# Row sums of a 32x512x1024 tensor: one or two loads issued ahead of the opening barriers

## Chip, cores and metric

The kernel runs on one core of a Trainium2 chip. The metric is the device time of one execution in microseconds (us). Before the change it is 160.77 us, the median of 3 runs (160.69 to 160.84).

## What is computed

```python
def reference(x: np.ndarray) -> np.ndarray:      # x: float32 (32, 512, 1024)
    return np.sum(x, axis=-1).astype(np.float32)
```

64 MB are read, 64 KB are written: 16,384 rows of 1024 numbers are summed, each to one number.

## The kernel before

The 16,384 rows are spread over 128 partitions, 128 rows for each, cut into three blocks of 32, 48 and 48 rows for a partition (`BLOCKS`). Within a block each partition's rows are contiguous in memory. A block is worked off in groups of 16 rows (`G`), eight groups in all, so a full group is a tile of 128 partitions x 16,384 numbers, 64 KB for a partition and 8 MB in all. Three such buffers (`xt`) are used in turn, so the load of group b+3 must wait until the sums of group b are done.

All loads are issued by SyncE (SP), from a list `loads` (L90 to L103) that is worked off in one loop (L146 to L149). The list begins with two loads for group 0: the first row alone (`LEAD`, 4 KB for a partition, 512 KB in all, semaphore `first`) and the other fifteen rows (60 KB for a partition, 7,680 KB, semaphore `slot0`). Groups 1 to 6 follow, one load each, and then the last group in smaller pieces: 9, 4 and 2 rows into its `xt` buffer, and its last row in two parts into `tail`. Group b's load, from b = 3 on, waits for VectorE's counter `vec` (L148). All these loads go through one DMA queue, and 16 DMA engines share each of them, 8 partitions to an engine.

VectorE sums the rows of a group with one `tensor_reduce` (L63): one row first (L110, after `first`), then the other fifteen of group 0 (L115, after `slot0`), then 16 at a time; ScalarE (L74) takes 7 rows of the seventh group and half of each of the last pieces. The last row is summed by two instructions at L81. The results leave by three stores (L155) and a last one (L159), issued by SP.

The program that is built has an entry part and a body. In the entry part GpSimd (POOL) sets four constants, and all engines meet in barriers (the profile gives the first of them L208, and two more L169): each engine drains, adds to a semaphore that Pool waits for, and then waits for Pool's release. The body, with everything above, comes behind them, after a branch. The end of the kernel (L175 to L194) edits this order by hand: it takes the first `EARLY` DMA instructions of SP out of the body and puts them in the entry part, ahead of SP's first drain:

```python
    loads = [i for i in code if i.engine == sp and i.opcode == "DMACopy"][:EARLY]
    for load in loads:
        assert not load.sync_info.on_wait
        code.remove(load)
    body.instructions = code
    code = list(entry.instructions)
    at = next(k for k, i in enumerate(code) if i.engine == sp and i.opcode == "Drain")
    code[at:at] = loads
```

With `EARLY = 2` these are the two loads of group 0.

Of the kernel before, what the change touches and what calls it, by code (L numbers as in the profile page):

```python
# [13 lines left out]
ACT_ROWS = 7  # L14
CUT = 544
CUTS = (0, 9, 13, 15)
EARLY = 2


def row_sums(nc, x: bass.AP, out: bass.AP):  # L20
# [146 lines left out]
def kernel(tc: tile.TileContext, x: bass.AP, out: bass.AP):  # L167
# [17 lines left out]
    code = list(body.instructions)  # L185
    loads = [i for i in code if i.engine == sp and i.opcode == "DMACopy"][:EARLY]
    for load in loads:
# [36 lines left out]
```

## Time and profile before

| what | value |
|---|---|
| median of 3 runs | 160.77 us |
| the profiled execution's own time | 160.73 us |
| its span in the trace | 159.4 us |
| read from memory | 67.11 MB, 421 GB/s over the span |
| one-row load, issue to landing | 3.5 us |
| 15-row load, issue to landing | 21.2 us |
| VectorE, sum of 16 rows (128x16,384) | 17.22 us |
| VectorE, sum of 15 rows | 16.15 us |
| VectorE's longest wait, for the 15-row load | 16.9 us |

The span runs from the first instruction in the trace, SP's first DMA issue, to the last one. SP's own column in the profile (SPq) shows how long it takes to issue a DMA; the transfer itself follows on the DMA engines, and "landing" is when its semaphore has its full count. An engine name with a q is that engine's sequencer, where waits and barriers are handled.

### The profile page before, as it was taken

How to read it: one execution, taken by the hardware profiler on the slowest of the kernel's cores; microseconds unless marked ns; L12 is line 12 of the kernel's file. 1: busy time of each engine (PE TensorE's matmuls, PEld its weight loads, DVE VectorE, ACT ScalarE, POOL GpSimd, SP SyncE). 2: the span in 40 equal slices, each digit the busy share in tenths (PEclk: the TensorE clock that was granted, in tenths of full speed). 3: DMA queues.
4: the chain of work that ended last, by engine and by line, in shares of the span. 5: the costliest groups of instructions: out<-in, count | busy, mean ns of one | idle time of the engine just before them, and what ended most of it. 6: DMA issues, size and time to landing. Idle time of an engine off the chain costs nothing.

```text
span 159.4 us, 110 instructions
## 1 busy us (share of the span) xinstructions
DVE 121.5 (76%) x17; ACT 17.2 (11%) x31; POOL 0.2 (0%) x4
## 2 busy tenths in 40 slices
DVE  1100059994799968999499994999949999499685
ACT  3000000000000000000000000000000000494694
POOL 0000000000000000000000000000000000000000
DMA  9988996996997989969969969969979799699994
GB/s 378 493 370 370 493 526 263 526 526 263 526 477 312 526 378 411 526 263 526 526 263 526 526 263 526 526 263 526 460 329 526 312 477 526 296 444 444 387 400 151
DMA packets 2448, 67.18 MB, mean 421 GB/s; under 512 B 784, under 2 KB 912, under 8 KB 1168
## 3 DMA queue, kind: packets, MB, share of 16 engines
q1 hardware_dynamic: 2448, 67.18, 98.2%
HBM read 67.11 MB, written 0.07 MB: 421 GB/s over the span
## 4 chain that ended last, share of the span: by engine, by line
DMA 75%; DVE 22%; SPq 1%; issue 0%
DMA xt<-in_x_dram 50%; DMA tail<-in_x_dram 25%; DVE res L63 22%; SPq L149 1%; DVE pairs L81 0%; DVE res L81 0%
## 5 line engine op out<-in xcount | busy, mean ns | idle before, releaser
L63 DVE TENSOR_REDUCE res<-xt 128x16 f32<-128x16384 f32 (+5 forms) x10 | 119.9, 11994 | 34.1 <-DMA xt<-in_x_dram 34.1
L74 ACT ACTIVATE xt<-xt 128x1024 f32<-128x1024 f32 x15 | 15.6, 1043 | 138.3 <-DMA xt<-in_x_dram 138.3
L74 ACT ACTIVATION_READ_ACCUMULATOR xt<-xt 128x1 f32 x15 | 2.8, 187 | 0.0
L107 DVE MEMSET tail<- 128x1 f32 x1 | 0.1, 59 | 2.0 <-PEq L169 2.0
L74 ACT ACT_TABLE_LOAD x1 | 1.3, 1283 | 1.9 <-PEq L169 1.9
L81 DVE CUSTOM_DVE_ANT_0 pairs<-tail 128x272 f32<-128x272 f32 (+1 forms) x2 | 0.9, 428 | 0.1
L81 DVE CUSTOM_DVE_ANT_0 pairs<-xt 128x512 f32<-128x512 f32 x1 | 0.7, 693 | 0.2 <-DMA xt<-in_x_dram 0.2
L81 DVE DVE_READ_ACCUMULATOR2_ANT res<- 128x1 f32 x2 | 0.2, 82 | 0.0
L208 POOL MEMSET const-bfloat16-1.0<- 128x1 bf16 x1 | 0.1, 102 | 0.0
L208 POOL MEMSET const-uint8-127<- 128x1 uint8 x1 | 0.1, 101 | 0.0
L208 POOL MEMSET const-float32-0.0<- 128x1 f32 x1 | 0.1, 99 | 0.2 <-issue 0.2
L208 POOL MEMSET const-float32-1.0<- 128x1 f32 x1 | 0.1, 98 | 0.0
L81 DVE DVE_READ_ACCUMULATOR2_ANT tail<- 128x1 f32 x1 | 0.1, 82 | 0.0
## 6 DMA issues: line engine op xcount, KB each, us to landing
xt<-in_x_dram SPq DMA_DIRECT2D x1, 7680.0 KB, 21.2
xt<-in_x_dram SPq DMA_DIRECT2D x1, 4608.0 KB, 32.6
xt<-in_x_dram SPq DMA_DIRECT2D x1, 2048.0 KB, 37.0
xt<-in_x_dram SPq DMA_DIRECT2D x1, 1024.0 KB, 39.0
xt<-in_x_dram SPq DMA_DIRECT2D x1, 512.0 KB, 3.5
tail<-in_x_dram SPq DMA_DIRECT2D x1, 272.0 KB, 39.2
tail<-in_x_dram SPq DMA_DIRECT2D x1, 240.0 KB, 39.3
xt<-in_x_dram SPq DMA_DIRECT2D x6, 40.8
```

What stands on the lines that cost most here:

```text
L63: nc.vector.tensor_reduce(out=res[:, c : c + n], in_=t[:, j * D : (j + n) * D].rearrange("p (j d) -> p j d", d=D), axis=X, op=ADD,).then_i ...
L74: nc.scalar.activation(out=v, in_=v, func=COPY, accum_out=res[:, c + i : c + i + 1]).then_inc(act, 1)
L81: nc.vector.tensor_tensor_reduce(out=pairs[:, 0 : h - a], in0=t[:, a:h], in1=t[:, h:b], scale=1.0, scalar=0.0, op0=ADD, op1=ADD, accum_out ...
L107: nc.vector.memset(tail[:, CUT + 15 : CUT + 16], 0.0).then_inc(vec, 1)
L149: nc.sync.dma_start(out=dst, in_=src).then_inc(s, 16)
L208: nc = _bacc.Bacc("TRN2", target_bir_lowering=False, num_devices=1)
```

## The change

```diff
-EARLY = 2
+EARLY = 1
```

Only the one-row load is now put ahead of SP's first drain. The 15-row load stays at the head of the body's loop, behind the barriers and the branch. SP's order becomes as follows; that of the other engines is unchanged:

```diff
 L149 DMACopy xt<-in_x_dram 128x1024
+L219 UnconditionalBranch
 L149 DMACopy xt<-in_x_dram 128x15360
-L219 UnconditionalBranch
 L149 DMACopy xt<-in_x_dram 128x16384 x6
 L149 DMACopy xt<-in_x_dram 128x9216
```

Nothing else is changed: sizes, buffers, semaphores and the order of the loads in the queue stay.

## The prediction

> **What bounds the kernel now.** I read the page's head and its DMA table, then the chain of waits in order of time, then the start of the timeline on SP's queue, then the barrier's instructions, and last the DMA engines in windows of 0.1 us around the first two loads. The page first:
>
> ```profile
> span 159.4 us, 110 instructions
> DVE 121.5 (76%) x17; ACT 17.2 (11%) x31; POOL 0.2 (0%) x4
> ...
> q1 hardware_dynamic: 2448, 67.18, 98.2%
> ```
>
> The one DMA queue keeps its 16 engines occupied for 98.2% of the span, VectorE is busy for 76%. The chain of waits says the same at both ends (start us, length us, what):
>
> ```profile
> 1.91 39.07 DMA xt<-in_x_dram
> ...
> 118.14 39.32 DMA tail<-in_x_dram
> 157.46 0.05 issue
> 157.51 0.41 DVE pairs L81
> 157.92 0.01 DVE res L81
> ```
>
> The last load lands at 157.46; VectorE needs 0.41 us more. So a microsecond in which the DMA engines stand empty at the start arrives at the end as a microsecond, unless something later absorbs it; and nothing does, because the loads stand in one queue back to back: the load of group 3 is issued when group 0 is reduced, at 37.8 us (15-row reduce from 21.64, 16.15 us long), while group 2 only begins to be reduced at 60.36 us. A re-issue is thus some 22 us ahead of the engines running dry.
>
> The change touches only the first three microseconds. Three looks at SP's queue, each ending at a different time (first row: up to 0.3 us, second: up to 1.0 us, third: 1.4 to 2.0 us):
>
> ```profile
> 0.00 0.38 SPq L149 DMA_DIRECT2D xt<-in_x_dram  x1
> 0.00 0.85 SPq L149 DMA_DIRECT2D xt<-in_x_dram  x2
> 1.91 0.33 SPq L149 DMA_DIRECT2D xt<-in_x_dram  x1
> ```
>
> The issue of the one-row load fills 0 to 0.38, that of the 15-row load ends at 0.85, and the next load is issued at 1.91, behind the barriers. The barrier's own instructions (durations in ns min/median/max, then first and last start in us):
>
> ```profile
> L208 POOLq EVENT_SEMAPHORE  x2: 17/17/17, 1.1 to 1.1; - x2
> ...
> L208 POOL MEMSET const-uint8-127<- x1: 101/101/101, 0.3 to 0.3; 128x1 uint8 x1
> L208 SPq DRAIN  x1: 125/125/125, 0.9 to 0.9; - x1
> ```
>
> Pool finishes its last memset at 0.43 and the other engines drain by 0.3; SP's drain at 0.9 is the last to arrive, behind the second DMA issue, and Pool releases the barrier just after it, at 1.1. The opening barrier therefore waits for exactly the issue that the change takes away.
>
> What the DMA engines do meanwhile (window, its length, busy of DVE, ACT, POOL, then clock, DMA share and GB/s; a packet is counted whole in the window in which it starts):
>
> ```profile
> 0.90:1.00 0.10, 0.00 (x0) 0.00 (x0) 0.00 (x0) 1.00 0.00 0
> 1.00:1.10 0.10, 0.00 (x0) 0.00 (x0) 0.00 (x0) 1.00 2.60 328
> ...
> 2.40:2.60 0.20, 0.00 (x0) 0.20 (x1) 0.00 (x0) 1.00 0.99 410
> 2.60:2.70 0.10, 0.00 (x0) 0.10 (x1) 0.00 (x0) 1.00 5.24 2171
> 2.70:2.80 0.10, 0.00 (x0) 0.10 (x1) 0.00 (x0) 1.00 10.38 4383
> 2.80:2.90 0.10, 0.00 (x0) 0.10 (x1) 0.00 (x0) 1.00 3.13 1311
> 2.90:3.00 0.10, 0.00 (x0) 0.10 (x1) 0.00 (x0) 1.00 4.27 1843
> 3.00:3.20 0.20, 0.00 (x0) 0.19 (x1) 0.00 (x0) 1.00 0.76 328
> ```
>
> The first packet of the one-row load starts at 1.0 us after its issue began at 0. A row of the 15-row load is 61,440 bytes for a partition, which shows as a jump of the GB/s column: 2171 GB/s for 0.1 us is 217 KB, three such packets and some rows of 4 KB. Read this way the 16 engines pass from the first load to the second 3, 7, 2, 3 and 1 at a time, in the windows at 2.65, 2.75, 2.85, 2.95 and 3.1 us (mean 2.80). Until then the one-row load covers the second one's set-up completely.
>
> **The change, step by step.**
>
> 1. Removed ahead of the barriers: one DMA issue on SP, 0.85 - 0.38 = 0.47 us with the gap before it. Pool is ready at about 0.48 (memset to 0.43; its own drain starts at 0.3 and takes 0.179), SP now drains from about 0.43 for 0.125 us, so SP is still last, but 0.47 us sooner, and the three barriers behind it follow rigidly: body code begins at 1.91 - 0.47 = 1.44 us. Bounds of this gain: 0 (something else holds the barriers) and 0.47; I take 0.47, since no other engine's row ends after 0.5.
>
> 2. Moved: the issue of the 15-row load, from 0.43 to 1.44 us. It has no semaphore wait of its own; it passes SP's drains, the three barriers and the branch into the body. Behind it on SP stand the loads of groups 1 and 2, which in the kernel before were issued at 1.91 and 2.29; now they come at 1.44 + 0.33 + 0.05 = 1.82 and, with 0.42 more, about 2.3. Their engines are busy with the 15-row load until about 20.8, so they cost nothing: cover 18 us.
>
> 3. From issue to packets. The one row for a load that meets idle engines is the first load: 1.0 us. Then the 15-row load's descriptors are at the engines from 1.44 + 1.0 = 2.44, some 0.1 to 0.3 us later at the last ones (the first load's packets also begin spread over 1.0 to 1.3). The engines come free from 2.6 to 3.1, mean 2.80. So each still finds its next packet, with 0.16 us to spare at the first and about 0.25 on the mean. Upper bound of the delay: a whole store at the end takes 1.4 us from issue to landing, data and receipt included; with 1.4 the packets come at 2.84, and the ten engines free by 2.75 wait (3 x 0.19 + 7 x 0.09)/16 = 0.08 us on the mean, 0.19 at worst. Idle: 0 to 0.19, I take 0.
>
> 4. Exposed start-up. In steady running 512 KB at the page's 421 GB/s take 1.25 us; the first load takes from 1.0 to 2.80 on the mean, so a cold start costs 0.55 us. In the kernel before, the second load had its descriptors in place long before and paid none of that. Now they come 0.25 us ahead on the mean. Bounds: 0 (work queued ahead hides it) and 0.55 - 0.25 = 0.30 (all of it is paid but for the head start). I take 0.10, nearer to zero since engines are still moving data when the new descriptors come, so they don't start from idle.
>
> 5. Gains. The second load's descriptors no longer arrive while the first load is running; if part of its 0.55 us was due to them, the first load ends sooner. Bounds 0 and 0.3; I take 0: no row separates this cause from a slow first access to memory, which would stay.
>
> 6. Elsewhere. VectorE's and ScalarE's first instructions (a memset and a table load of 1.28 us) start 0.47 us sooner and are hidden: VectorE waits for the first row until 3.53 and for the 15 rows until 21.64 anyway. If that cover were gone they would cost under 1.3 us, but it is 16.9 us wide. The 1.33 us outside the span (160.73 - 159.40) stay.
>
> Sum: 160.73 + 0 + 0.10 = 160.83 us on the profiled run's own time; the median of the runs is 160.77, 0.04 above that run, so I predict **160.9 us**, a change of about +0.1 us, less than 0.2% (0.32 us), which is about what a measurement of this kernel can tell from no change.
>
> In the Trainium skill, DMA: Bandwidth & Descriptors, Latency and other measured facts, a DMA issued from SP has its first byte after about 0.6 us. The first load's 1.0 us is longer, so the trace doesn't bear that out here; by an estimate from that page's figure the packets would be there at 2.04, far ahead, and the time would be 160.8.
>
> **Rivals.**
>
> *The queue runs dry (slower).* The place is the handover at 2.6 to 3.1 us; it decides once descriptors plus first data come later than the engines come free, that is from 0.25 us of delay beyond step 3. For it: the head start is small, and the first load shows 0.55 us of start-up per engine. Against it: 1.0 us may itself be the cold price of a first issue. If the whole start-up is paid after an idle of 0 to 0.19, the cost is 0.35 to 0.75: about 161.3.
> The same page of the Trainium skill (Rules for kernel authors) tells to issue a DMA early so that its fixed set-up overlaps with other work, which speaks against this change; the rows show that the overlap here shrinks to 0.25 us.
>
> *The barriers don't move up.* Were the release not held by SP, the issue would be at 1.91 and packets at 2.91: idle (3 x 0.26 + 7 x 0.16 + 2 x 0.06)/16 = 0.13 us with all engines served at once, some 0.1 more with their spread, and 0.1 to 0.3 of start-up: +0.3 to +0.5, about 161.15. Against it stands SP's drain, the last before the release.
>
> *The first load gains (faster).* If the second load's descriptors are what slows the first, it ends up to 0.3 to 0.5 us sooner, and the second follows at 2.44 at once: 2.80 - 2.44 = 0.36 at most, 160.4. For it: the first load's excess; against: an engine's first access is slow in any case.
>
> **How the numbers follow.** Forecast (covered, or nearly): 0.44, of which 0.40 stay within 0.2%, 0.03 are slower, 0.01 faster; own range 160.6 to 161.1. Queue dry: 0.36 (0.33 slower, 0.03 within). Barriers unmoved: 0.10 (0.08 slower, 0.02 within). First load gains: 0.10 (0.07 faster, 0.03 within). Together faster 0.08, same 0.48, slower 0.44. The range 160.5 to 161.5 takes in the forecast, the unmoved barriers and most of the dry queue, and leaves out the largest gain and the dearest restart, about 0.15.
>
> **What would show it.** SP's second issue at 1.44 (step 1; 1.91 for the second rival); the jump of GB/s still spread over 2.6 to 3.1 (steps 3 and 4; later and bunched together if the queue ran dry, earlier if the first load gained); the 15-row reduce at 21.6 to 21.8; the last landing and the end later by the same amount as that reduce. I am wrong if the handover moves by over 0.3 us, or if the handover holds and the end moves.

## The result, and the profile after

The changed kernel takes 162.58 us, the median of 6 runs (162.12 to 163.44), beside 160.81 us (160.69 to 161.06) for the kernel before in the same runs: a ratio of 1.011, with a 95% interval of 1.0096 to 1.0125. It is slower by 1.8 us, and it scatters: 1.3 us between its runs where the kernel before has 0.4. The profiled execution took 162.82 us, 2.09 more than the one before.

The page after, first its head and the DMA queue:

```profile
span 161.5 us, 110 instructions
DVE 121.5 (75%) x17; ACT 17.2 (11%) x31; POOL 0.2 (0%) x4
...
q1 hardware_dynamic: 2448, 67.18, 97.5%
```

The work is the same to the instruction, the packet and the megabyte; VectorE's busy time is still 121.5 us. The queue's share went from 98.2% to 97.5%, so the DMA engines stood empty for longer (an estimate from share and span: 4.0 us instead of 2.9). The chain of waits, from where the 15-row load is issued and at the end:

```profile
1.43 0.33 SPq L149
...
120.31 39.24 DMA tail<-in_x_dram
159.55 0.04 issue
159.59 0.41 DVE pairs L81
160.00 0.01 DVE res L81
```

The last load lands at 159.55 instead of 157.46; behind it nothing has changed (VectorE 0.41 us). The barrier's instructions (ns min/median/max, first and last start in us) and VectorE's first reductions in the timeline:

```profile
L208 POOLq EVENT_SEMAPHORE  x2: 17/17/17, 0.6 to 0.7; - x2
...
L208 SPq DRAIN  x1: 131/131/131, 0.4 to 0.4; - x1
```

```profile
3.60 1.22 DVE L63 TENSOR_REDUCE res<-xt 128x1 f32<-128x1024 f32 x1 [2.03 <-DMA xt<-in_x_dram]
23.54 16.15 DVE L63 TENSOR_REDUCE res<-xt 128x15 f32<-128x15360 f32 x1 [18.72 <-DMA xt<-in_x_dram]
```

SP drains at 0.4 instead of 0.9, and the body's first issue is at 1.43 instead of 1.91. Yet the 15-row reduction begins at 23.54 instead of 21.64: 1.90 of the 2.1 us are lost before the second load has landed. The first row's reduction is at 3.60 as against 3.53, so the loss lies behind the first load. The DMA windows show it (us, length, busy of DVE, ACT, POOL, clock, DMA share, GB/s):

```profile
2.80:2.90 0.10, 0.00 (x0) 0.00 (x0) 0.00 (x0) 1.00 0.71 287
2.90:3.00 0.10, 0.00 (x0) 0.00 (x0) 0.00 (x0) 1.00 0.32 123
3.00:3.20 0.20, 0.00 (x0) 0.00 (x0) 0.00 (x0) 1.00 2.20 656
3.20:3.40 0.20, 0.00 (x0) 0.00 (x0) 0.00 (x0) 1.00 5.69 1843
3.40:3.60 0.20, 0.00 (x0) 0.00 (x0) 0.00 (x0) 1.00 3.61 1229
3.60:4.00 0.40, 0.40 (x1) 0.00 (x0) 0.00 (x0) 1.00 0.00 0
4.00:4.20 0.20, 0.20 (x1) 0.00 (x0) 0.00 (x0) 1.00 2.44 922
4.20:4.40 0.20, 0.20 (x1) 0.00 (x0) 0.00 (x0) 1.00 0.85 307
```

A packet of 61,440 bytes counts as 307 GB/s in a window of 0.2 us, so the 16 engines begin the second load 2, 6, 4, 3 and 1 at a time, from 3.05 to 4.30 us; before, they did so from 2.61 to 3.17. They had finished the first load at 2.7 to 3.2, so most of them stood dry, and four for about a microsecond. The share column tells a second thing: in the row at 3.2, 5.69 x 0.2 us x 16 engines = 18.2 us for six packets, 3.0 us each. In the trace's packet records the first packet of the second load takes 2.93 us on the mean of the engines, 2.32 before and 2.27 in steady running: the second load starts slowly, as the first one did (called a cold start below). This is not simply what an idle engine pays: of the four engines that begin after 4.0 us, dry the longest, two take only 2.27.

Three terms, all from the packet records, make up the 1.90 us: the second load begins later by 0.71 us on the mean of the engines (3.52 against 2.81), of which 0.53 is idle time, since they finished the first load at 2.99 on the mean (the rest is the first load's own end, at 2.79 before); its first packet takes 0.62 us longer; and the engines now finish it spread over 1.28 us instead of 0.52, so that the last of them, for which VectorE waits, is 0.86 behind the mean instead of 0.27, another 0.59. Together 1.92, to 0.03 us. Nothing gives this back: the last of the engines finishes the last load 2.02 us later than before, and the spread is still 0.99 us there (0.46 before).

### The profile page after: what moved, and what is told of

It is laid out like the page before. It is cut to its first block, busy times and chain, and to the rows that moved or that the text cites. A ratio compares the mean times of both kernels' runs of the same rounds, so it can differ in the third digit from the quotient of the medians.

```text
span 161.5 us, 110 instructions
## 1 busy us (share of the span) xinstructions
DVE 121.5 (75%) x17; ACT 17.2 (11%) x31; POOL 0.2 (0%) x4
## 3 DMA queue, kind: packets, MB, share of 16 engines
q1 hardware_dynamic: 2448, 67.18, 97.5%
## 4 chain that ended last, share of the span: by engine, by line
DMA 75%; DVE 22%; SPq 1%; issue 0%
DMA xt<-in_x_dram 51%; DMA tail<-in_x_dram 24%; DVE res L63 21%; SPq L149 1%; DVE pairs L81 0%; DVE res L81 0%
```

## The experiments

The theory after the result: a load that is issued while another one is running reaches the engines not 1.0 us but up to 3 or 4 us after its issue (the time from the start of its issue to an engine's first packet of it is called its delivery below); if the work ahead of it ends sooner, they run dry and the load starts cold. Its rivals: the load suffers from where it is issued (the body, behind the branch), from the two issues that follow it at once, from SP's queue, or from any second load whatever the engines do. Each edit is given against the changed kernel.

**More work ahead.** Four rows in the early load, twelve in the one behind the barriers (the same edit with 2 and 3 rows comes below):

```diff
-LEAD = 1
+LEAD = 4
...
-    loads = [(0, xt[0][:, 0:D], x_0[:, 0:D], sems["first"])]
-    loads.append((0, xt[0][:, D : G * D], x_0[:, D : G * D], slots[0]))
+    loads = [(0, xt[0][:, 0 : LEAD * D], x_0[:, 0 : LEAD * D], sems["first"])]
+    loads.append((0, xt[0][:, LEAD * D : G * D], x_0[:, LEAD * D : G * D], slots[0]))
```

> Theory (the queue runs dry): behind the barriers the second load's packets come 1.6 to 2.9 us after its issue, while the one-row load covers it only until 2.7 to 3.2 us. With four rows in the early load (2 MB, busy until about 6 us) the second load's first packets follow without a gap, all 16 within some 0.6 us, each 2.0 us or shorter for its twelve rows, and the time is that of the kernel before, 160.8 us (160.5 to 161.1). Rival (a load issued behind the barriers streams worse whatever stands ahead of it): the time stays at 162 us or more.

Measured: 160.80 us, ratio to the kernel before 0.9997 (0.9988 to 1.0006). The second load is issued at 1.43 us as in the changed kernel, and its first packets follow the first load's last ones at 6.5 to 6.9 us without a gap. The place of the issue, behind barriers and branch, costs nothing by itself; with enough work ahead to cover the delivery, the whole loss is gone.

**Idle engines.** SP waits for the first load before it issues the second:

```diff
-    for b, dst, src, s in loads:
+    for k, (b, dst, src, s) in enumerate(loads):
+        if k == 1:
+            nc.sync.wait_ge(sems["first"], 16)
```

> SP waits for the one-row load to land (3.6 us) before it issues the 15-row load, so that the engines stand idle. If packets are late because the engines are busy with the first load: the first packet 1.0 us after the issue, the 16 within 0.3 us, and with a second cold start of 0.6 us the time is the one before + (4.7 - 2.8) + 0.6 = 163.3 us. If they are late because of the two issues that follow at once, or because it is the second load: again 1.6 to 2.9 us after the issue, first packets from 5.2 to 6.5 us, time 164.0 to 164.8 us.

Measured: 163.43 us, ratio 1.0155 (1.0139 to 1.0172). The issue in the timeline, and the windows behind it:

```profile
3.55 1.28 SPq L151 DMA_DIRECT2D xt<-in_x_dram  x3
```

```profile
3.60:4.40 0.80, 0.80 (x1) 0.00 (x0) 0.00 (x0) 1.00 0.00 0
4.40:4.60 0.20, 0.20 (x1) 0.00 (x0) 0.00 (x0) 1.00 7.64 2458
4.60:4.80 0.20, 0.18 (x1) 0.00 (x0) 0.00 (x0) 1.00 7.76 2458
4.80:5.00 0.20, 0.00 (x0) 0.00 (x0) 0.00 (x0) 1.00 0.00 0
```

2458 GB/s is eight packets, twice: all 16 engines begin between 4.51 and 4.75 us, 0.96 to 1.21 us after the issue. So with idle engines a second load needs the 1.0 us of the first one, though two more issues follow it at once here too. What this load pays besides its later issue is the cold start: 7.64 x 0.2 x 16 / 8 = 3.06 us for a packet that takes 2.27 in steady running, 0.8 us too long, more than the 0.67 of the changed kernel (2.93 against 2.27).

**The next issues later.** Groups 1 and 2 are issued only after the first reduction:

```diff
-    for b, dst, src, s in loads:
+    for k, (b, dst, src, s) in enumerate(loads):
+        if k == 2:
+            nc.sync.wait_ge(vec, 2)
```

> The loads of groups 1 and 2 are issued only after VectorE's first reduce (4.8 us), nothing else differs from the changed kernel. If their issues at 1.81 and 2.29 us delay the 15-row load's packets: these come 1.0 us after their issue, the handover is at 2.6 to 3.1 us as in the kernel before, time 160.9 us. If not: first packets again from 3.0 to 4.3 us, time 162.1 to 163.4 us.

Measured: 162.91 us, ratio 1.0139 (1.0111 to 1.0167). The first packets come from 2.88 to 4.39 us, as in the changed kernel (3.05 to 4.30). The issues behind the load are not what delays it.

**Nothing early.** `EARLY = 0`: both loads behind the barriers.

> No load ahead of the barriers; both loads of group 0 are issued back to back behind them. Theory: only one cold start, and the second load's packets follow without a gap; the barriers open as soon as Pool is ready (about 0.5 us), the first issue comes about 1.3 us after the engines begin, time 160.8 + 1.3 = 162.1 us, so about the changed kernel's own: the early one-row load brings hardly anything when the next load is not in the queue behind it. Rival (the changed kernel loses by the place of the 15-row load alone): both costs add, 163.5 us or more.

Measured: 162.27 us, ratio 1.0097 (1.0077 to 1.0117). The first issue is at 1.38 us, its packets begin 1.0 us later, and the second load, issued 0.43 us behind it, follows without a gap and with no long first packet. With the intervals as they are, this can't be told from the changed kernel: one row put ahead of the barriers alone brought nothing.

**The second load between the barriers.** Both loads are taken out of the body as before, but the second is put back ahead of SP's first, or of its last, drain there:

```diff
-EARLY = 1
+EARLY = 2
...
+    drains = [k for k, i in enumerate(code) if i.engine == sp and i.opcode == "Drain"]
+    code.insert(drains[0], loads.pop())
     body.instructions = code
```

The second run has `drains[-1]` in place of `drains[0]`.

> The 15-row load is issued after the first barrier and ahead of the other two, at about 0.8 us (before: 0.43, changed: 1.43). If delivery takes 1.45 to 2.9 us once the first load's traffic runs: its first packets from about 2.6 to 3.7 us, only the latest engines run dry, time 161.0 to 161.6 us. If a load needs 1.0 us whenever it is issued and the changed kernel's loss came from the body or the branch: no gap, 160.8 us.

> The 15-row load is issued after the second barrier, at about 1.1 us. If delivery takes 1.45 to 2.9 us: first packets from 2.7 to 4.0 us, about half of the changed kernel's loss or more, 161.6 to 162.3 us. If the loss came from the body or the branch: 160.8 us.

Measured: issued at 0.78 us, 161.53 us, ratio 1.0052 (1.0025 to 1.0078), with single runs from 160.64 to 162.90 (one more, of 163.12, is not in the ratio): some executions lose nothing, and the profiled one (160.81) is such a one, without a gap. 0.78 us is on the edge. Issued at 1.11 us, 163.16 us, ratio 1.0141 (1.0116 to 1.0166): above the 161.6 to 162.3 expected, and no better than the issue at 1.43. Its windows:

```profile
2.40:2.60 0.20, 0.00 (x0) 0.20 (x1) 0.00 (x0) 1.00 2.54 1024
2.60:2.80 0.20, 0.00 (x0) 0.20 (x1) 0.00 (x0) 1.00 4.01 1659
2.80:3.00 0.20, 0.00 (x0) 0.20 (x1) 0.00 (x0) 1.00 0.72 307
3.00:3.80 0.80, 0.48 (x1) 0.14 (x1) 0.00 (x0) 1.00 0.00 0
...
4.20:4.40 0.20, 0.20 (x1) 0.00 (x0) 0.00 (x0) 1.00 1.65 614
4.40:4.60 0.20, 0.14 (x1) 0.00 (x0) 0.00 (x0) 1.00 1.60 614
4.60:4.80 0.20, 0.00 (x0) 0.00 (x0) 0.00 (x0) 1.00 1.59 614
4.80:5.00 0.20, 0.00 (x0) 0.00 (x0) 0.00 (x0) 1.00 0.83 307
5.00:5.20 0.20, 0.00 (x0) 0.00 (x0) 0.00 (x0) 1.00 8.66 2765
```

Eight engines pass to the second load by 3.0 us without a gap. Seven more begin at 4.2 to 4.9 us, up to 3.8 us after the issue; the nine packets that start at 5.0 to 5.2 are the last engine's first one and the second ones of the eight, and they take 8.66 x 0.2 x 16 / 9 = 3.1 us each. So delivery is not the same for all engines: behind one row, too, it can take up to 3.9 us. And engines that did keep running have long packets as well, once the others have started, so idle time alone does not explain a long packet.

**Two and three rows early.**

> Changed kernel with two rows in the early load (1 MB, engines busy until 4.0 to 4.4 us). Delivery of the second load by 2.9 to 4.4 us is then covered on all engines but perhaps the last, no second cold start: 160.8 to 161.2 us. If an engine whose queue has nothing else in it always restarts cold, however long the load ahead was: about 0.6 us of first-packet excess again, 161.4 us or more.

> Changed kernel with three rows in the early load (1.5 MB, engines busy until about 5.4 us). Two rows left engines dry between 4.0 and 5.5 us, four rows none (busy until 6.7). If delivery ends at some fixed time of about 4 us after the issue (5.5 us) whatever runs: only the last one or two engines wait, time 160.8 to 161.3 us. If delivery stretches with the traffic ahead of it: again several engines dry after 5.4 us and first packets 0.5 us too long, 161.6 to 162.3 us.

Measured: two rows 162.10 us, ratio 1.0073 (1.005 to 1.0096), against the expectation of full cover; three rows 160.72 us, ratio 0.9989 (0.998 to 0.9998). With two rows the engines are free from 3.9 to 4.3 us and the second load reaches them from 3.87 to 5.51, up to 4.1 us after its issue at 1.45:

```profile
4.20:4.40 0.20, 0.00 (x0) 0.00 (x0) 0.00 (x0) 1.00 0.83 287
4.40:4.60 0.20, 0.00 (x0) 0.00 (x0) 0.00 (x0) 1.00 0.00 0
4.60:4.80 0.20, 0.15 (x1) 0.00 (x0) 0.00 (x0) 1.00 1.73 573
4.80:5.00 0.20, 0.20 (x1) 0.00 (x0) 0.00 (x0) 1.00 1.68 573
5.00:5.20 0.20, 0.20 (x1) 0.00 (x0) 0.00 (x0) 1.00 0.83 287
5.20:5.40 0.20, 0.20 (x1) 0.00 (x0) 0.00 (x0) 1.00 0.86 287
5.40:5.60 0.20, 0.20 (x1) 0.00 (x0) 0.00 (x0) 1.00 0.80 287
```

Here a first packet is 287 GB/s: single engines still begin at 5.4 us. With three rows the first load ends at 5.3 to 5.7 us (3.9 to 4.3 us after the issue):

```profile
5.20:5.40 0.20, 0.00 (x0) 0.00 (x0) 0.00 (x0) 1.00 1.38 594
5.40:5.60 0.20, 0.00 (x0) 0.00 (x0) 0.00 (x0) 1.00 6.17 2663
5.60:5.80 0.20, 0.00 (x0) 0.00 (x0) 0.00 (x0) 1.00 2.47 1065
```

A first packet of 53,248 bytes is 266 GB/s here: 2, 10 and 4 engines pass to the second load, none waits, and none of these packets is long (6.17 x 0.2 x 16 / 10 = 1.97 us, as in steady running). Of the two cases expected for three rows, the first one came: delivery was done by about 4 us after the issue, and it did not stretch on with the traffic. Behind two rows it took up to 4.1 us; behind one row up to 2.9 with the issue at 1.43, but up to 3.9 with the issue at 1.11. That it grows with the amount of data ahead is therefore not shown, only that it is long while a load is running.

**Another queue.** The 15-row load is issued on ScalarE's queue, at the same moment; SP's next issue waits for the first reduction:

```diff
+    nc.scalar.dma_start(out=loads[1][1], in_=loads[1][2]).then_inc(slots[0], 16)
...
+        if s is slots[0] and b == 0:
+            nc.sync.wait_ge(vec, 2)
+            continue
```

> The 15-row load goes through ScalarE's own queue, issued at the same 1.44 us; SP issues groups 1 and 2 only after VectorE's first reduce. If delivery is slow because the 16 engines and their path are busy with the first load: first packets again 1.45 to 2.9 us after the issue, engines dry around 3.2 us, time 162 to 163.5 us. If it is slow because SP's queue still holds the one-row load: first packets 1.0 to 1.3 us after the issue, no engine dry, 160.8 to 161.2 us.

Measured: 162.28 us, ratio 1.0092 (1.0068 to 1.0117). Issued at 1.44 us, the first packets come from 2.85 to 3.85, that is 1.4 to 2.4 us later, and take 0.64 us too long:

```profile
2.80:3.00 0.20, 0.00 (x0) 0.20 (x1) 0.00 (x0) 1.00 2.73 922
3.00:3.20 0.20, 0.00 (x0) 0.12 (x1) 0.00 (x0) 1.00 6.34 2150
3.20:3.40 0.20, 0.07 (x1) 0.00 (x0) 0.00 (x0) 1.00 4.61 1536
...
3.80:4.00 0.20, 0.20 (x1) 0.00 (x0) 0.00 (x0) 1.00 0.89 307
```

That is 3, 7, 5 and 1 first packets of 307 GB/s. SP's own queue is not the cause. It fits what the Trainium skill says (DMA: Bandwidth & Descriptors, Issuing engines are not separate DMA queues): loads that different engines issue run on the same 16 DMA engines.

**Less work ahead.** A quarter of a row early, the rest behind the barriers, group 0 summed in one instruction:

```diff
-    loads = [(0, xt[0][:, 0:D], x_0[:, 0:D], sems["first"])]
-    loads.append((0, xt[0][:, D : G * D], x_0[:, D : G * D], slots[0]))
+    loads = [(0, xt[0][:, 0 : D // 4], x_0[:, 0 : D // 4], sems["first"])]
+    loads.append((0, xt[0][:, D // 4 : G * D], x_0[:, D // 4 : G * D], slots[0]))
...
-    rows_dve(xt[0], 0, LEAD, groups[0][1], 0)
...
-        j = LEAD if b == 0 else 0
+        j = 0
```

> Changed kernel with only a quarter of a row in the early load (128 KB, done by about 1.6 to 1.9 us), so that the engines are nearly idle when the next load is issued at 1.43 us; VectorE sums group 0 in one instruction. If running traffic is what delays delivery: the second load's first packets come 1.0 to 1.3 us after the issue, from 2.4 to 2.8 us, all engines at once, with a cold start of 0.8 us; the end 161.9 to 162.5 us, no later than with a whole row early although a quarter of the data goes ahead. If delivery takes 1.6 to 2.9 us in any case: first packets from 3.0 to 4.3 us and 163.0 to 164.0 us.

Measured: 161.78 us, ratio 1.0059 (1.0046 to 1.0073), a little better than expected and faster than a whole row early. The first load is done at 1.4 to 1.7 us, and the second one, issued at 1.43 in the same place, begins at 2.39 to 2.99, most engines at once:

```profile
2.20:2.40 0.20, 0.00 (x0) 0.20 (x1) 0.00 (x0) 1.00 0.96 323
2.40:2.60 0.20, 0.00 (x0) 0.20 (x1) 0.00 (x0) 1.00 10.49 3548
2.60:2.80 0.20, 0.00 (x0) 0.12 (x1) 0.00 (x0) 1.00 1.88 645
2.80:3.00 0.20, 0.00 (x0) 0.00 (x0) 0.00 (x0) 1.00 1.57 645
```

A packet counts as 323 GB/s here: 1, 11, 2 and 2 engines, 1.0 to 1.6 us after the issue. Same place, same queue, same issues behind it: what differs is the traffic ahead (besides three quarters of a row more in the second load and the missing sum of the first row), and with it the delay.

**One load for the whole group.** One early issue as in the changed kernel, but of all 16 rows, and one reduction of 16 rows:

```diff
-    loads = [(0, xt[0][:, 0:D], x_0[:, 0:D], sems["first"])]
-    loads.append((0, xt[0][:, D : G * D], x_0[:, D : G * D], slots[0]))
+    loads = [(0, xt[0][:, :], x_0[:, 0 : G * D], slots[0])]
...
-    nc.vector.wait_ge(sems["first"], 16)
-    rows_dve(xt[0], 0, LEAD, groups[0][1], 0)
...
-        j = LEAD if b == 0 else 0
+        j = 0
```

> One DMA issue ahead of the barriers as in the changed kernel, but for all 16 rows of group 0 at once, no separate first row; VectorE sums group 0 in one instruction of 17.2 us. No handover at 3 us, the next load is issued at 1.43 us with 20 us to spare: the time of the kernel before, 160.8 us, or up to 0.2 us less, and as steady. If the early one-row load were worth something by itself, as an early start of VectorE: slower than before by up to 1 us.

Measured: 160.80 us, ratio 0.9998 (0.9989 to 1.0007). VectorE's early first row is worth nothing, since VectorE isn't the bound; a single early issue is enough if it is large.

The delivery of the second load side by side, from the packet records of one execution each (all in us; "too long" is against a packet of the same load in steady running):

| kernel | second issue | first load done | its first packets | after the issue | first packet too long by | median |
|---|---|---|---|---|---|---|
| before | 0.43 | 2.6 to 3.2 | no gap | hidden | 0.05 | 160.81 |
| changed | 1.43 | 2.7 to 3.2 | 3.05 to 4.30 | 1.6 to 2.9 | 0.67 | 162.58 |
| quarter row early | 1.43 | 1.4 to 1.7 | 2.39 to 2.99 | 1.0 to 1.6 | 0.60 | 161.78 |
| idle engines | 3.55 | 2.8 to 3.2 | 4.51 to 4.75 | 1.0 to 1.2 | 0.81 | 163.43 |
| between the barriers | 1.11 | 2.5 to 2.9 | 2.60 to 5.00 | up to 3.9 | 0.24 | 163.16 |
| two rows early | 1.45 | 3.9 to 4.3 | 3.87 to 5.51 | up to 4.1 | 0.45 | 162.10 |
| three rows early | 1.45 | 5.3 to 5.7 | no gap | hidden | 0.00 | 160.72 |

## Why the prediction failed, step by step

The prediction was 160.9 us, in a range to 161.5; it came out at 162.58. The sign that it named as its refutation, the handover moving by over 0.3 us, came: it moved by 0.71.

1. The barriers: right. SP's drain was the last to arrive; without the second issue the body began 0.47 us sooner, with SP's issue at 1.43 us (1.44 predicted).
2. The order of the queue: right. Groups 1 and 2, issued at 1.81 and 2.29, cost nothing.
3. From issue to packets: **this step failed.** It took 1.0 us from the one load that met idle engines, and 1.4 us from a whole store as the upper bound, and so found the descriptors at the engines at 2.44 us with 0.16 to 0.25 us to spare. The 1.0 us holds for idle engines (0.96 to 1.21 us) and not behind a running load, where it took 1.6 to 2.9 us. Both rows that I bounded it by were transfers with little or nothing ahead of them. The kernel before had no row for this: its second load was issued at 0.43 us, before any packet ran, its later loads stood far ahead of their turn, and whatever delivery they took was hidden; the range should have been open upwards there.
4. The exposed start-up: wrong in size, by way of step 3. With no head start more of it is paid than the 0.10 taken: the first packets are 0.62 us longer than before, and 0.8 longer than in steady running from fully idle engines, against the whole 0.55 that the prediction reckoned with. I also reckoned with the mean over the engines; the engines' spread, which went from 0.52 to 1.28 us, adds 0.59, because a load has landed only when its slowest engine is done.
5. No gain for the first load: right, it ended 0.19 us later on the mean (2.99 against 2.79), not sooner.
6. What lies elsewhere: right, VectorE's and ScalarE's sooner start was hidden, and 1.3 us still lie outside the span.

The rival of the dry queue was the right mechanism and the right place. It was priced at 161.3 us, from an idle of 0 to 0.19 us and 0.35 to 0.75 us in all (its own terms, 0.55 and the idle time, add up to 0.55 to 0.74), where the idle time alone was 0.53 on the mean, and the spread was not in it. The unmoved barriers and the faster first load fell. The Trainium skill's rule to issue a DMA early (DMA: Bandwidth & Descriptors, Rules for kernel authors), set beside that rival, held between 0.43 and 1.43 us; the issue at 1.11 us gained nothing over 1.43. The Trainium skill's first byte after about 0.6 us (the same page, Latency and other measured facts) fits the traces after all where the engines are idle, if it is counted from the end of SP's issue and not, as the prediction did, from its start: the first load's issue ends at 0.38 and its first packet starts at 1.01 us in the kernel before, 0.63 later, and with the second load issued to idle engines it is 3.88 and 4.51 us. Behind a running load it is 1.3 to 2.5 us, from 1.76 to 3.05 and 4.30 in the changed kernel.

What stays open: by what path running traffic delays a later load, why some engines are served at once and others up to 2 us later, why half of the engines were served later with the issue at 1.11 us than with that at 1.43, and why packets are long after a restart, on engines that never ran dry too. The runs exclude the queue, the issues behind the load and the place in the program as the cause of the delay, not more.

## What to carry to other kernels

A kernel whose DMA queue is its bound should not let it run empty, and the first handover is where that happened here: what is issued ahead of a barrier has to be large enough to cover the next load's delivery at its length under load (here 4 us, 1.5 MB, three rows), or the next load had better be issued ahead of the barrier too. A delay that the trace hides behind other work has an unknown length; don't take it from a transfer that met idle engines. And reckon with the slowest of the 16 engines, not with their mean.

## Not expected

A load's delivery depends on whether another load is running: 1.0 to 1.2 us with idle engines, 1.6 to 2.9 behind one row (512 KB) in the changed kernel, up to 3.9 or 4.1 in other runs behind one or two. So less data issued early was faster: a quarter of a row ahead of the barriers gave 161.78 us (ratio 1.0059), a whole row 162.58 (1.011). Once the 16 engines have been pulled apart, the spread stays: with the second load issued at 1.11 us it was 2.3 us at its landing and still 2.3 us six loads later.
